# Regrouping the shifted inputs of a state-space stage: a DRAM round trip of five DMAs on GpSimd's queue in place of sixteen identity products per block

## The chip, the cores and the metric

The kernel runs on one core of one Trainium2 chip. The metric is the device time of one launch in microseconds (us). Each version is run several times, and its median is taken. One further execution is recorded by the hardware profiler; the rows below come from it.

## The reference, cut to what matters

Two layers of a decoder trunk on 256 tokens of width 2048, all in float32: layer 0 mixes tokens by stick-breaking attention, layer 1 by a state-space layer (S5), and each is followed by a squared-ReLU MLP. The change lies in the S5 layer alone:

```python
u = h @ w_in                                  # 256 x 2048
ug = u.reshape(B, S, S5_GROUPS, S5_GROUP)     # 128 groups of 16 channels
bur = einsum('btgc,gpc->btgp', u_chunk, bbr)  # and bui: 64 complex states per group
pr, pi, sr, si = associative_scan(combine, (a_r, a_i, bur, bui), axis=1)
y = einsum('btgp,gcp->btgc', hr, cr) - einsum('btgp,gcp->btgc', hi, ci)
y = y + d_skip * u
z = gelu(y)
a, g = split(z @ w_glu, 2)
return a * sigmoid(g)
```

## The kernel before

Activations lie with channels on the partitions: a block is 128 channels (8 S5 groups) by 256 tokens, and there are 16 blocks. The recurrence is not run token by token but in chunks of 4 tokens: the state is updated once per chunk from the chunk's four inputs, and the outputs inside a chunk are made from that state and from short taps on the inputs. For this the inputs of a block are wanted in another form, the tile `imc`: the partition is 32 j + p (p: one of 32 channels of a quarter q; j: the shift in the chunk), and the free dimensions are q (4) and chunk k (65, with one zero column for the chunk before the first).

The stage is `s5_mixer`. Its outer loop runs 8 times over a pair of blocks (`gi`). An iteration multiplies four weight tiles of w_in (`cols_tile`: 24 matmuls each, every weight split into a high and a low part by ScalarE, L130, and VectorE, L132). After each weight tile comes a `tick`, and at a tick the work planned for it by `at(delay, ...)` is issued in the order in which it was planned. So the S5 work of a block is strung over later ticks, between the weight tiles. For block b of a pair, with t = 4 + 2 b counted from the start of the pair:

- t: `s5_expand` (spreads the coefficients, and loads T on SyncE's queue) and `s5_windows`: VectorE takes the finished product out of PSUM times the RMS row (L974), ScalarE adds the shift (L975), both into the tile `u`.
- t + 1: `s5_operands` (L953, L960 on TensorE) and `s5_shuffle`: 16 matmuls with 32 columns of the identity (each runs as two instructions) read `u` in steps of 4 tokens and put the four shifts onto the four partition groups of a PSUM bank (L983). ScalarE copies the bank to `imc` (L985).
- t + 2: `s5_states`: 8 matmuls on `imc` (L998, 16 instructions), then six elementwise operations and one scan on VectorE (L1000 to L1008), giving the states R.
- t + 4: `s5_taps`.
- t + 6: `s5_outputs`: matmuls on R and on `imc` (L1023), then VectorE adds d times u to the product, in `u` (L1024), and ScalarE applies gelu (L1027) into `z`.

Ticks of even and of odd number therefore alternate: at an even tick stand the outputs of one block, the taps of the next and the states of the one after; at an odd tick the operands and the shuffle. `u` and `imc` have three buffers each, so the `u` of a block is free when the gelu of the block three before, issued at the same tick, has read it.

TensorE and GpSimd keep the order in which the program is written (`manual_schedule`). For ScalarE, VectorE and SyncE a scheduler decides the order when the program is compiled. Beside the stage's own work, VectorE has filler: weighted sums for the adaLN vectors of the next sub-layers (L348, L350), on weights `adaw` that SyncE loads. After the stage the GLU follows, whose last weight tiles need the `z` of all 16 blocks (split at L121 and L122); `flush` then issues what is still planned.

Of the kernel before, what the change touches and what calls it, by code (L numbers as in the profile page):

```python
# [8 lines left out]
F32 = mybir.dt.float32  # L9
# [3 lines left out]
AF = mybir.ActivationFunctionType  # L13
OP = mybir.AluOpType
AX = mybir.AxisListType

P = 128
D = 2048
NB = D // P
S = 256  # L20
# [36 lines left out]
class Trunk:  # L57
# [793 lines left out]
    def s5_open(self, sp):  # L851
        g_ = self.nc.gpsimd
        self.sE = sp.tile([P, 2, 4, 4, 2, 16], F32, name="E")
        self.sCA = [sp.tile([P, 2, 4, 4, 2, 16], F32, name="CA%d" % k) for k in range(3)]
        self.sKL = [sp.tile([P, 3, 4, 2, 16], F32, name="KL%d" % k) for k in range(3)]
        self.simc = [sp.tile([P, 4, 65], F32, name="imc%d" % k) for k in range(3)]
        self.sU = [sp.tile([P, 4 + S + 1], F32, name="u%d" % k) for k in range(3)]
        self.sM = [sp.tile([P, 2, 4, 64], F32, name="M%d" % k) for k in range(2)]
        self.sP = [sp.tile([P, 224], F32, name="taps%d" % k) for k in range(2)]
        for t in [self.sE] + self.sP + self.sM + self.sCA + [u[:, 0:4] for u in self.sU]:  # L860
            g_.memset(t, 0.0)
        self.sS = {}

# [104 lines left out]
            nc.tensor.transpose(pk[:, tau * P - P:tau * P], self.sP[bi % 2][:, o:o + P], self.ident)  # L968
        nc.scalar.activation(self.sKL[bi % 3].rearrange("p t q a e -> p (t q a e)"), pk[:, :3 * P], AF.Copy)

    def s5_windows(self, bi, acc):
        nc = self.nc
        uw = self.sU[bi % 3]
        nc.vector.tensor_tensor(uw[:, 4:], acc[:, :S + 1], self.rms, op=OP.mult)  # L974
        nc.scalar.activation(uw[:, 4:4 + S], uw[:, 4:4 + S], AF.Identity, bias=uw[:, 4 + S:])  # L975

    def s5_shuffle(self, bi):
        nc = self.nc
        uw, imc = self.sU[bi % 3], self.simc[bi % 3]
        pi = self.mp()  # L980
        for q in range(4):
            for j in range(4):
                nc.tensor.matmul(pi[32 * j:32 * j + 32, 65 * q:65 * q + 65], self.ident[:, 32 * q:32 * q + 32],  # L983
                                 uw[:, 4 - j:4 - j + 257:4], start=True, stop=True)
        nc.scalar.activation(imc.rearrange("p q k -> p (q k)"), pi[:, :4 * 65], AF.Copy)  # L985

    def s5_states(self, sp, bi):
        nc, s5 = self.nc, self.s5
# [20 lines left out]

    def s5_outputs(self, sp, bi):  # L1010
        nc = self.nc
        u, St = self.sU[bi % 3][:, 4:4 + S], self.sS.pop((bi, "R")).rearrange("p c (q k) -> p c q k", q=4)
        CA, KL, imc = self.sCA[bi % 3], self.sKL[bi % 3], self.simc[bi % 3]
        py = self.mp()
        for tau in range(4):
            for c in range(2 if tau == 0 else 3):
                for q in range(4):
                    o = py[32 * q:32 * q + 32, 64 * tau:64 * tau + 64]
                    if c < 2:
                        lhs, rhs = CA[:, c, q, tau], St[:, c, q]  # L1020
                    else:
                        lhs, rhs = KL[:, tau - 1, q], imc[:, q, 1:65]
                    nc.tensor.matmul(o, lhs.rearrange("p a e -> p (a e)"), rhs, start=(c == 0), stop=(c == (2 if tau else 1)))  # L1023
        nc.vector.scalar_tensor_tensor(u.rearrange("p (k i) -> p i k", i=4), u.rearrange("p (k i) -> p i k", i=4),  # L1024
                                       self.dcol[:, bi:bi + 1], py[:, 0:S].rearrange("p (i k) -> p i k", i=4),
                                       op0=OP.mult, op1=OP.add)
        nc.scalar.activation(self.z[:, bi], u, AF.Gelu_apprx_tanh)  # L1027
        if not self.split_z:
            self.sdone.add(bi)
        else:  # L1030
            self.split(self.hH[:, bi, :S], self.hL[:, bi, :S], self.z[:, bi])

    def s5_mixer(self, mid):
        nc, tc = self.nc, self.tc
        w_in, w_glu = self.i["s5_w_in"][0], self.i["s5_w_glu"][0]
        st = ExitStack()
        sp = st.enter_context(tc.tile_pool(name="s5", bufs=1, reuse_waits="tile"))
        self.z = sp.tile([P, NB, S], F32, name="z")
        self.split_z, self.sdone = False, set()
        hH, hL = self.h()  # L1040
        self.at(1, self.rms_stat, self.sq)
        self.at(3, self.rms_rows)
        self.s5_open(sp)
        self.s5_load(sp, 0)
        for gi in range(8):
            acc = self.accs()
            if gi < 7:
                self.at(2, self.s5_load, sp, gi + 1)
            for b in range(2):
                bi = 2 * gi + b  # L1050
                t = 4 + 2 * b
                self.at(t + 6, self.s5_outputs, sp, bi)
                self.at(t - 0, self.s5_expand, sp, bi)
                self.at(t, self.s5_windows, bi, acc[:, b])
                self.at(t + 1, self.s5_operands, sp, bi)
                self.at(t + 1, self.s5_shuffle, bi)
                self.at(t + 2, self.s5_states, sp, bi)
                self.at(t + 4, self.s5_taps, bi)
            for t in range(4):
                self.cols_tile(acc, w_in, gi * 256, t, hH, hL)  # L1060
        self.open_h(self.pers)
        z = self.h(S)
        for bi in range(16):
            if bi in self.sdone:
                self.split(self.hH[:, bi, :S], self.hL[:, bi, :S], self.z[:, bi])
        self.split_z = True
        self.pace(44, mid[-1])
        sq = self.new_sq()

        def before():  # L1070
            self.flush()
            st.close()
            self.open_h(self.ctx.enter_context(tc.tile_pool(name="h1", bufs=1, reuse_waits="tile")))

        for _ in range(1):
            self.tick()
        a, b = self.gemm_two(w_glu, D, 0, *z, before)
        with tc.tile_pool(name="glu", bufs=2, reuse_waits="tile") as gp:
            for g in range(8):
                if g:  # L1080
                    a = self.gemm_cols(w_glu, D + g * 256, *z)
                sg = gp.tile([P, 2, S], F32, name="sg")
                nc.scalar.activation(sg, a[:, :, :S], AF.Sigmoid)
                if g:
                    b = self.gemm_cols(w_glu, g * 256, *z)
                nc.vector.tensor_tensor(sg, b[:, :, :S], sg, op=OP.mult)
                if g == 5:
                    self.drain(*mid)
                    self.shifts(0, 16, 1, 1)
                    for kb in range(10):  # L1090
                        self.fold(kb, 1, 1)
                for j in range(2):
                    self.residual(sg[:, j], 2 * g + j, 1, 2, sq)
                    if g > 4:
                        self.fold(2 * g + j, 1, 1)
        self.sq = sq
# [128 lines left out]
```

## Time and profile before

| what | us |
|---|---|
| median of 3 runs | 2493.76 (2490.83 to 2493.91) |
| profiled execution, time | 2488.38 |
| profiled execution, span of the trace | 2486.6 |
| TensorE busy | 2374.3 |
| VectorE busy | 1830.0 |
| ScalarE busy | 1207.1 |
| GpSimd busy | 255.6 |

The span is what the trace covers; 1.8 us of the profiled time lie around it. Busy time of an engine is the time in which at least one of its instructions ran; a TensorE that is busy throughout can still be working at less than its fastest, as its matmuls overlap. In the rows, PE is TensorE, PEld its weight loads, DVE is VectorE, ACT ScalarE, POOL GpSimd and SP SyncE; a "q" after the name means the engine's sequencer.

### The profile page before, as it was taken

The numbers are of one execution on the slowest core, as the hardware profiler recorded it, in microseconds if no ns is written. First come the engines' busy times: TensorE is split into PE (matmuls) and PEld (weight loads), VectorE is DVE, ScalarE is ACT, GpSimd is POOL, SyncE is SP. The second block draws the span as 40 slices with busy tenths as digits, with TensorE's granted clock in tenths as the row PEclk, the third lists the DMA queues.
The fourth block names the chain that finished last, engine by engine and source line by source line (L and its number), as shares of the span: only waits on it lengthen the run. The fifth ranks groups of instructions, "written<-read, shape, count | busy, mean of one in ns | idle before, by whom it ended". The sixth has DMA issues, their size and how long they took to land.

```text
span 2486.6 us, 48432 instructions
## 1 busy us (share of the span) xinstructions
PE 2374.3 (95%) x19843; PEld 2234.8 (90%) x19843; DVE 1830.0 (74%) x2479; ACT 1207.1 (49%) x1806; POOL 255.6 (10%) x292
## 2 busy tenths in 40 slices
PE   7999999999999888988999999999999999999998
PEld 4776789899999778888999998999999999999998
DVE  5699999999888878787797699658555555555543
ACT  4534875355444234433546676444543543543543
POOL 0000100000003444454400000000000000000000
PEclk9999999999999989999999999999999999999999
DMA  9898899999998888888898577768555655655654
GB/s 337 301 309 301 289 315 320 334 309 317 320 306 286 274 269 276 262 287 282 279 312 304 179 240 228 230 186 280 177 181 186 184 183 185 185 184 184 185 184 140
DMA packets 503058, 627.28 MB, mean 252 GB/s; under 512 B 44434, under 2 KB 374580, under 8 KB 500532
## 3 DMA queue, kind: packets, MB, share of 16 engines
q1 hardware_dynamic: 499776, 609.31, 75.1%
q0 software_dynamic: 2432, 14.68, 1.5%
q8 instruction: 155, 2.54, 0.4%
q14 instruction: 67, 0.55, 0.1%
q10 hardware_dynamic: 628, 0.21, 0.0%
HBM read 607.34 MB, written 16.78 MB: 251 GB/s over the span
## 4 chain that ended last, share of the span: by engine, by line
PE 58%; DVE 13%; issue 10%; DMA 9%; POOL 7%; ACT 2%; SPq 0%; ACTq 0%; DVEq 0%; POOLq 0%
PE acc L159 14%; PE acc L161 14%; PE acc L160 14%; DMA adaw<-in_ada_w 5%; DVE wl L132 4%; PE acc L145 3%; PE acc L146 3%; PE acc L147 3%; DVE adacc L350 3%; DMA rot<-turns 2%; DVE adsums L350 2%; DMA w<-in_mlp_w 2%; PE mp L291 1%; PE mp L322 1%; ACT wh L130 1%
## 5 line engine op out<-in xcount | busy, mean ns | idle before, releaser
L130 ACT ACTIVATE wh<-w 128x1024 fp32r<-128x1024 f32 x736 | 777.5, 1058 | 1052.9 <-PE acc L161 544.6
L132 DVE TENSOR_TENSOR wl<-w,wh 128x1024 fp32r<-128x1024 f32 x736 | 914.9, 1245 | 409.3 <-ACT wh L130 408.3
L159 PE MATMUL acc<-hH,wl 128*128 128x258 f32 (+1 forms) x2816 | 808.1, 287 | 33.7 <-DVE wl L132 32.2
L161 PE MATMUL acc<-hH,wh 128*128 128x258 f32 (+1 forms) x2816 | 799.5, 284 | 0.0
L160 PE MATMUL acc<-hL,wh 128*128 128x258 f32 (+1 forms) x2816 | 798.0, 283 | 0.5 <-DVE hL L122 0.5
L159 PE MATMUL acc<-aH,wl 128*128 128x256 f32 x2048 | 587.4, 287 | 39.1 <-DVE wl L132 38.4
L160 PE MATMUL acc<-aL,wh 128*128 128x256 f32 x2048 | 581.6, 284 | 0.0
L161 PE MATMUL acc<-aH,wh 128*128 128x256 f32 x2048 | 581.6, 284 | 0.0
L159 PEld LDWEIGHTS acc<-hH,wl 128*128 128x128 f32 x2816 | 535.9, 190 | 48.7 <-DVE wl L132 38.3
L160 PEld LDWEIGHTS acc<-hL,wh 128*128 128x128 f32 x2816 | 536.6, 191 | 0.7 <-DVE hL L122 0.7
L161 PEld LDWEIGHTS acc<-hH,wh 128*128 128x128 f32 x2816 | 535.1, 190 | 0.0
L159 PEld LDWEIGHTS acc<-aH,wl 128*128 128x128 f32 x2048 | 391.0, 191 | 48.5 <-DVE wl L132 47.1
L160 PEld LDWEIGHTS acc<-aL,wh 128*128 128x128 f32 x2048 | 391.1, 191 | 0.0
L161 PEld LDWEIGHTS acc<-aH,wh 128*128 128x128 f32 x2048 | 391.0, 191 | 0.0
L350 DVE SCALAR_TENSOR_TENSOR adacc<-adaw,cond,adacc 128x512 f32<-128x512 f32 x390 | 296.9, 763 | 22.5 <-DMA adaw<-in_ada_w 19.2
L350 DVE SCALAR_TENSOR_TENSOR adsums<-adaw,cond,adsums 128x512 f32<-128x512 f32 x270 | 216.1, 802 | 30.5 <-DMA adaw<-in_ada_w 26.5
L145 PE MATMUL acc<-wh,hL 128*128 128x512 f32 x384 | 156.8, 408 | 5.8 <-ACT wh L130 3.1
L146 PE MATMUL acc<-wl,hH 128*128 128x512 f32 x384 | 153.6, 400 | 3.4 <-DVE wl L132 3.3
L147 PE MATMUL acc<-wh,hH 128*128 128x512 f32 x384 | 152.6, 398 | 0.0
L145 PEld LDWEIGHTS acc<-wh,hL 128*128 128x128 f32 x384 | 73.3, 191 | 32.3 <-issue 13.7
L146 PEld LDWEIGHTS acc<-wl,hH 128*128 128x128 f32 x384 | 72.9, 190 | 21.2 <-DVE wl L132 6.3
L147 PEld LDWEIGHTS acc<-wh,hH 128*128 128x128 f32 x384 | 73.0, 190 | 17.0
(288 smaller groups left out, 2068.9 us busy)
## 6 DMA issues: line engine op xcount, KB each, us to landing
w<-in_mlp_w SPq DMA_DIRECT2D x512, 512.0 KB, 3.9
adaw<-in_ada_w SPq DMA_DIRECT2D x384, 512.0 KB, 5.8
w<-in_sb_w_in SPq DMA_DIRECT2D x96, 512.0 KB, 5.5
w<-in_s_w_glu SPq DMA_DIRECT2D x64, 512.0 KB, 3.9
w<-in_sb_w_out SPq DMA_DIRECT2D x32, 512.0 KB, 5.6
w<-in_s_w_in SPq DMA_DIRECT2D x32, 512.0 KB, 4.6
pw<-W POOLq DMA_DIRECT2D x8, 1024.0 KB, 4.2
W<-pw SPq DMA_DIRECT2D x8, 1024.0 KB, 6.7
```

The source lines that it names most:

```text
L130: nc.scalar.activation(h, w, AF.Copy)
L132: nc.vector.tensor_tensor(l, w, h.bitcast(F32), op=OP.subtract)
L145: nc.tensor.matmul(o, aL(kb)[:, s], H[:, kk], start=(kb == k0), stop=False)
L146: nc.tensor.matmul(o, aH(kb)[:, s], L[:, kk], start=False, stop=False)
L147: nc.tensor.matmul(o, aH(kb)[:, s], H[:, kk], start=False, stop=(kb == k1 - 1))
L159: nc.tensor.matmul(o, L[:, kk, s], aH(kb), start=(kb == k0), stop=False)
L160: nc.tensor.matmul(o, H[:, kk, s], aL(kb), start=False, stop=False)
L161: nc.tensor.matmul(o, H[:, kk, s], aH(kb), start=False, stop=(kb == k1 - 1))
L291: nc.tensor.matmul(st["bank"][32 * kk:32 * kk + 32], self.cond32[:, 4 * t + kk], pair[kk // 2][:, kk % 2], start=(t == 0), stop=(t == 3))
L322: nc.tensor.matmul(st["bank"][32 * i:32 * i + 32], self.ones[:, 0:32], acc, start=True, stop=True)
L350: nc.vector.scalar_tensor_tensor(acc, wt[:, kk], c, acc, op0=OP.mult, op1=OP.add)
```

## The change

The 16 identity products and the copy out of PSUM go. `s5_inputs` takes the place of `s5_windows` and `s5_shuffle`: VectorE writes the scaled product into a tile `uw` of its own; ScalarE, while adding the shift, writes it into `u` with the four tokens of a chunk apart (position first, chunk second). GpSimd's queue stores `u` to a DRAM tile `um` (16 of them, one per block), and four reads on the same queue bring back position (4 - j) mod 4 into the 32 partitions of shift j of `imc`, the shifted ones one column later. The zero columns of `imc` are now set once, by a memset of the three buffers. Since `u` now lies position first, L1024 works on contiguous data, and the gelu writes its result in steps of four tokens. `s5_states` moves from t + 2 to t + 3.

```diff
@@ s5_open
-        self.sU = [sp.tile([P, 4 + S + 1], F32, name="u%d" % k) for k in range(3)]
+        self.sU = [sp.tile([P, S], F32, name="u%d" % k) for k in range(3)]
+        self.um = [self.dram.tile([P, S], F32, name="um%d" % bi) for bi in range(16)]
...
-        for t in [self.sE] + self.sP + self.sM + self.sCA + [u[:, 0:4] for u in self.sU]:
+        for t in [self.sE] + self.sP + self.sM + self.sCA + self.simc:
             g_.memset(t, 0.0)
@@
-    def s5_windows(self, bi, acc):
-        nc = self.nc
-        uw = self.sU[bi % 3]
-        nc.vector.tensor_tensor(uw[:, 4:], acc[:, :S + 1], self.rms, op=OP.mult)
-        nc.scalar.activation(uw[:, 4:4 + S], uw[:, 4:4 + S], AF.Identity, bias=uw[:, 4 + S:])
-
-    def s5_shuffle(self, bi):
-        nc = self.nc
-        uw, imc = self.sU[bi % 3], self.simc[bi % 3]
-        pi = self.mp()
-        for q in range(4):
-            for j in range(4):
-                nc.tensor.matmul(pi[32 * j:32 * j + 32, 65 * q:65 * q + 65], self.ident[:, 32 * q:32 * q + 32],
-                                 uw[:, 4 - j:4 - j + 257:4], start=True, stop=True)
-        nc.scalar.activation(imc.rearrange("p q k -> p (q k)"), pi[:, :4 * 65], AF.Copy)
+    def s5_inputs(self, sp, bi, acc):
+        nc = self.nc
+        uw, u, imc = sp.tile([P, S + 1], F32, name="uw", bufs=1), self.sU[bi % 3], self.simc[bi % 3]
+        nc.vector.tensor_tensor(uw, acc[:, :S + 1], self.rms, op=OP.mult)
+        nc.scalar.activation(u.rearrange("p (i k) -> p i k", i=4), uw[:, :S].rearrange("p (k i) -> p i k", i=4), AF.Identity, bias=uw[:, S:])
+        nc.gpsimd.dma_start(self.um[bi], u)
+        src = self.um[bi].rearrange("(q p) (i k) -> i p q k", q=4, i=4)
+        for j in range(4):
+            o = 1 if j else 0
+            nc.gpsimd.dma_start(imc[32 * j:32 * j + 32, :, o:o + 64], src[(4 - j) % 4])
@@ s5_outputs
-        u, St = self.sU[bi % 3][:, 4:4 + S], self.sS.pop((bi, "R")).rearrange("p c (q k) -> p c q k", q=4)
+        u, St = self.sU[bi % 3], self.sS.pop((bi, "R")).rearrange("p c (q k) -> p c q k", q=4)
...
-        nc.vector.scalar_tensor_tensor(u.rearrange("p (k i) -> p i k", i=4), u.rearrange("p (k i) -> p i k", i=4),
-                                       self.dcol[:, bi:bi + 1], py[:, 0:S].rearrange("p (i k) -> p i k", i=4),
-                                       op0=OP.mult, op1=OP.add)
-        nc.scalar.activation(self.z[:, bi], u, AF.Gelu_apprx_tanh)
+        nc.vector.scalar_tensor_tensor(u, u, self.dcol[:, bi:bi + 1], py[:, 0:S], op0=OP.mult, op1=OP.add)
+        nc.scalar.activation(self.z[:, bi].rearrange("p (k i) -> p i k", i=4), u.rearrange("p (i k) -> p i k", i=4), AF.Gelu_apprx_tanh)
@@ s5_mixer
-                self.at(t, self.s5_windows, bi, acc[:, b])
+                self.at(t, self.s5_inputs, sp, bi, acc[:, b])
                 self.at(t + 1, self.s5_operands, sp, bi)
-                self.at(t + 1, self.s5_shuffle, bi)
-                self.at(t + 2, self.s5_states, sp, bi)
+                self.at(t + 3, self.s5_states, sp, bi)
                 self.at(t + 4, self.s5_taps, bi)
```

## Rows read from the trace of the kernel before

**Rows 1.** Stretches: from:to, us, busy us (instructions) per engine, granted clock, DMA share, GB/s
```profile
1357.00:1446.00 89.00, 89.00 (x1375) 81.73 (x1378) 59.94 (x78) 64.41 (x128) 0.00 (x0) 1.00 0.56 180
1446.00:1545.00 99.00, 97.55 (x1708) 89.46 (x1697) 96.33 (x152) 72.52 (x159) 0.00 (x0) 1.00 0.76 247
1545.00:1572.00 27.00, 25.36 (x425) 24.27 (x424) 25.33 (x37) 10.57 (x15) 0.00 (x0) 0.94 0.84 255
```
**Rows 2.** Timeline of TensorE over one block: start us, us, line, out<-in, count
```profile
1431.04 0.65 PE L953 MATMUL mp<-E,CA 128*32 128x128 f32 x16
1432.64 1.13 PE L983 MATMUL mp<-u,ident 128*32 128x65 f32 x32
1433.69 0.39 PE L159 MATMUL acc<-hH,wl 128*128 128x258 f32 x1
...
1436.77 0.65 PE L1023 MATMUL mp<-R,CA 128*32 128x64 f32 x32
1438.52 1.90 PE L998 MATMUL mp<-imc,VL 128*128 128x64 f32 x16
1440.23 0.37 PE L159 MATMUL acc<-hH,wl 128*128 128x258 f32 x1
...
1443.27 0.62 PE L322 MATMUL mp<-adsums,ones 128*32 128x512 f32 x2
```
**Rows 3.** Source line L983: ns min/median/max, first and last start
```profile
L983 PEldq EVENT_SEMAPHORE  x15: 51/51/51, 1371.4 to 1541.4; - x15
```
**Rows 4.** Timeline of ScalarE and VectorE around the same even tick [idle before <-releaser]
```profile
1439.11 0.68 DVE L1024 SCALAR_TENSOR_TENSOR u<-u,colv,mp 128x256 f32<-128x256 f32 x1
1439.83 0.42 ACT L1027 ACTIVATE z<-u 128x256 f32<-128x256 f32 x1
1442.11 0.51 ACT L975 ACTIVATE u<-u 128x256 f32<-128x256 f32 x1 [1.42 <-DVE u L974]
```
**Rows 5.** Timeline of TensorE and ScalarE at an even tick of the later blocks
```profile
1487.10 0.65 PE L1023 MATMUL mp<-R,CA 128*32 128x64 f32 x32
1491.05 0.42 ACT L1027 ACTIVATE z<-u 128x256 f32<-128x256 f32 x1 [0.59 <-DVE u L1024]
```
**Rows 6.** Timeline of GpSimd in the MLP before: a store, and the instruction that waits for it
```profile
806.33 0.62 POOL L849 DMA_DIRECT2D rot<-turns  x1 [0.31 <-POOL turns L848]
813.47 1.05 POOL L745 TENSOR_TENSOR turns<-s5lo,s5hi 128x256 f32<-128x256 f32 x1 [5.85 <-DMA rot<-turns]
```
**Rows 7.** DMA issues of the whole span: count, KB each, median us to landing
```profile
rot<-turns POOLq DMA_DIRECT2D x16, 384.0 KB, 5.3
T<-rot SPq DMA_DIRECT2D x16, 384.0 KB, 3.8
out<-ot SPq DMA_DIRECT2D x8, 256.0 KB, 2.5
```
**Rows 8.** Tile C (loads of 256-byte runs, 64 KB each, on SyncE's queue): time to landing
```profile
DMA to landing us min/median/max: 2.6/4.0/5.2
```
**Rows 9.** Source lines L418, L1024 and L849: ns min/median/max, first and last start
```profile
L418 DVE SCALAR_TENSOR_TENSOR xT<-acc,mod,xT x112: 469/476/486, 407.7 to 2481.9; 128x256 f32<-128x256 f32 x112
L1024 DVE SCALAR_TENSOR_TENSOR u<-u,colv,mp x16: 667/683/699, 1390.1 to 1564.3; 128x256 f32<-128x256 f32 x16
L849 POOL DMA_DIRECT2D rot<-turns x16: 606/615/623, 806.3 to 1234.1; - x16
```
**Rows 10.** Timeline of SyncE's queue and of VectorE: what the load of T waits for
```profile
1432.32 0.68 DVE L1007 TENSOR_TENSOR w<-R,T 128x512 f32<-128x512 f32 x1
1433.04 0.34 SPq L945 DMA_DIRECT2D T<-rot  x1
```
**Rows 11.** Timeline at the end of the stage: TensorE and VectorE
```profile
1558.75 0.68 DVE L1008 TENSOR_TENSOR R<-w,w 128x512 f32<-128x512 f32 x1
1561.04 0.65 PE L1023 MATMUL mp<-R,CA 128*32 128x64 f32 x32
1565.94 0.38 PE L159 MATMUL acc<-hH,wl 128*128 128x256 f32 x1 [1.14 <-ACT hH L121]
```

## The prediction

> **What bounds the kernel now.** I read the page's busy times first, then the stretches of the S5 stage, then TensorE's timeline inside one block, and last the chain that leads into the work that is moved.
>
> In the stretch of the first seven blocks TensorE is busy for 89.00 of 89.00 us, at the full granted clock, and VectorE for 59.94 [rows 1]. In the stretch of the nine later ones TensorE is busy for 97.55 of 99.00 and VectorE for 96.33: the adaLN filler runs there [rows 1]. So the first part is bound by TensorE alone; in the second VectorE stands close behind. GpSimd does nothing in either.
>
> The reader should see in [rows 2] that a block costs TensorE a fixed sequence with no waits. Even tick: outputs and taps, 1436.77 to 1438.52 (1.75 us), states to 1440.23 (1.71), a weight tile to 1443.27 (3.04). Odd tick: operands 1431.04 to 1432.64 (1.60), the shuffle to 1433.69 (1.05), a weight tile to 1436.77 (3.08). The sum is 12.23 us a block.
>
> **The change, part by part.** The identity products: 16 blocks x 1.05 us of start to start = 16.8 us of TensorE, all on the path. This is the whole of the possible gain that TensorE's rows show.
>
> ScalarE and VectorE: the copy out of PSUM goes (ScalarE, off the path: 64.41 of 89.00 us busy [rows 1]). The gelu and the shift become strided on one side. No row shows a ScalarE operation with steps of four elements; L1024 is one on VectorE, 0.683 us against 0.476 for the same operation on contiguous data [rows 9]. If ScalarE paid the same 0.21 twice it would give back about what the copy cost; at best nothing. I take nothing, under the cover of its idle 28%. L1024 becomes contiguous: about 0.21 less on VectorE per block, 1.9 us in the nine later blocks, where that can count. The memset of `imc` falls on GpSimd while it is idle; were it exposed it would cost about a microsecond once. TensorE's PSUM ring loses one of seven uses per block, which only loosens it.
>
> The new waits: the first state matmul must now wait for four DMAs instead of one ScalarE instruction. A wait that stands as an instruction of its own on TensorE's sequencer took 51 ns [rows 3]. Between none exposed and four per block: 0 to 16 x 4 x 0.051 = 3.3 us; I take 1, as the weight loads run ahead of the matmuls. Behind that wait stands everything on TensorE: the operands of the next block, the next weight tile, and behind these ScalarE's and VectorE's splits.
>
> The DRAM round trip, step by step. ScalarE ends the shift, GpSimd wakes (0.31 [rows 6]), issues the store, waits until it has landed, wakes, issues four reads about 0.65 apart (0.62 each [rows 6]), and the last must land.
> - Store. The nearest row is the other store from GpSimd's queue, three times as large: a median of 5.3 us to landing [rows 7], and 813.47 - 806.33 = 7.1 from the start of the issue to the instruction that waited [rows 6]. A store of twice the bytes from SyncE landed in 2.5 [rows 7]. Bounds 2.5 to 7.1; I take 4.5, nearer to GpSimd's, less something for the bytes.
> - Reads. The nearest row is the loads of 256-byte runs, the same runs as here: 2.6, 4.0 and 5.2 us [rows 8]. I take 4.0.
> - Sum: 0.3 + 4.5 + 0.3 + 3 x 0.65 + 4.0 = 11.05 us; bounds 0.3 + 2.5 + 0.3 + 1.95 + 2.6 = 7.65 and 0.3 + 7.1 + 0.3 + 1.95 + 5.2 = 14.85.
>
> What hides it: the distance from the end of the shift (even tick t) to the states (odd tick t + 3). On TensorE without the shuffle, from the start of the even tick: 1.75 + 3.04, then the odd tick of the block before, 1.71 + 1.60 + 3.08, then 1.75 + 3.04: 15.97 us. The shift can't start before the gelu of three blocks earlier has freed `u`. In the first part that gelu ends at 1440.25, 3.48 after the start of the even tick at 1436.77 [rows 2, 4]; with 0.51 for the shift itself the round trip starts at about 4.2, and 11.8 us are left. In the later blocks the gelu ends 4.37 after it [rows 5], the round trip starts at about 5.1, and 10.9 are left. A shortfall x is not paid in full at each block: the round trip of a block contains the stall of the block before and its own, so each stalls by x / 2. At 11.05 that is 0 in the first seven, and (11.05 - 10.9) / 2 = 0.08 in nine: 0.7 us. At the upper bound it is 7 x 1.5 + 9 x 2.0 = 28.5 us; at the lower bound 0.
>
> Is GpSimd held up when it issues? In the trace an issue there took 0.606 to 0.623 us in all 16 cases [rows 9], in stretches with VectorE at work, so nothing there looks like an issue that was held up. The Trainium skill, "SBUF — State Buffer", section "SBUF: two separate sides", says that DMAs from GpSimd have their descriptors written by that engine, and that certain VectorE operations shut it out meanwhile, so that the DMA seems to hang. By that rule the sum would hold a wait of up to one VectorE operation at each issue; it stands below as a rival.
>
> SyncE: the load of T waits for the last reader of T two blocks before; it went out at 1433.04, as that reader, L1007, ended (1432.32 + 0.68) [rows 10]. With the states one tick later it goes out some 5 us later, and the weight loads behind it on SyncE may too. T is not wanted for another block, and the weights are loaded three tiles ahead, some 6 us a tile. Nothing, unless the compiled order puts T ahead of a late weight: then up to those 5 us once or twice, which I keep for the range.
>
> Later blocks on VectorE: if their filler stays as it is, VectorE needs 96.33 / 99.00 x 12.23 = 11.90 us a block, less 0.21 = 11.69, and TensorE 11.18. Then a block gains 0.54 instead of 1.05, and nine give back 4.6 us. The filler is put in where the compiler sees room, so with shorter blocks less of it should stand there. Between 0 and 4.6 I take 2.
>
> The end of the stage: the states of the last block, too, come one tick later, but its outputs don't. L1008 of that block ended at 1559.43 and the outputs ran at 1561.04 [rows 11], 1.6 us of slack. A tick there is 3 us of TensorE, so the outputs wait 1.4 more, up to 3 with filler in between; the GLU's last tiles already waited 1.14 for the split of `z` behind them [rows 11]. I take 1.5.
>
> Sum: -16.8 + 1.0 + 0.7 + 2.0 + 1.5 = -11.6 us. Against the profiled execution: 2488.4 - 11.6 = 2476.8. The median of the runs lies 5.4 above it, so the median forecast is 2493.8 - 11.6 = 2482.2 us, say 2482.
>
> **The rivals.**
> - The round trip is half hidden. For it: five DMAs in two dependent steps, where one such store alone has taken 7.1 us. Against it: that store was three times the size, in a busier stretch. At 13 us the stalls are 7 x 0.6 + 9 x 1.05 = 13.7 in place of 0.7; with the later blocks held by TensorE's stalls the filler costs nothing more (-2): -11.6 + 13.0 - 2 = about -1, 2493.
> - The round trip is not hidden, and the kernel is slower. Place: the first state matmul of each block. It decides from the point where the stalls pass 14.3 us in all (16.8 less the 2.5 of waits and tail), about 0.9 a block: a round trip over 11.3 + 1.8 = 13.1 us on average. At the upper bound of 14.85 the sum is -16.8 + 1.0 + 28.5 + 1.5 = +14, 2508.
> - GpSimd's issues are held up by VectorE, one operation of about 0.7 us [rows 9] at each of the five: 3.5 us more, a round trip of 14.55, stalls of (7 x 2.75 + 9 x 3.65) / 2 = 26 us, +12, 2506. The even issue times speak against it. It is what the rule of the Trainium skill, above, would make of this kernel.
> - VectorE holds the later blocks in full: 4.6 in place of 2, and the tail at 3: -16.8 + 1 + 0.7 + 4.6 + 3 = -7.5, 2486.
>
> **How the numbers follow.** Hidden, as in the sum: 0.45. VectorE holds the later blocks: 0.15. Half hidden: 0.20. Not hidden: 0.15. Held-up issues: 0.05. The forecast is that of the likeliest, 2482. Upwards the range reaches through the half-hidden case to where the last two begin to weigh, 2500; downwards to the case in which nothing is given back (16.8) and VectorE's 1.9 counts, 2475. A difference of 0.2% (5 us) is about what can be told from none here. Faster by more than that: 0.45 + 0.15 less a little for misses of size, 0.57; within it: most of the half-hidden case, 0.20; slower: 0.23.
>
> **What would show it.** If right: TensorE's timeline shows operands followed directly by the weight tile and about 11.2 us a block in the first part; the four reads land before the first state matmul, and no wait of L998 on `imc` stands among the waits. If wrong by the round trip: TensorE idle in front of L998 with a DMA as releaser, of similar size at each block. If wrong by VectorE: L159 waiting for `wl` in the later blocks only. If wrong by held-up issues: DMA issues on GpSimd well over 0.62 us, or long gaps between issue and first byte beside VectorE's operations.

## The result, and the profile after

| kernel | median, us | lowest to highest |
|---|---|---|
| before | 2493.84 | 2490.83 to 2495.97 |
| changed | 2508.36 | 2501.04 to 2510.51 |

The changed kernel takes 1.0052 times as long as the one before (95% interval 1.004 to 1.0064), that is 14.5 us more, where 11.6 less was forecast. Its profiled execution has a span of 2508.2 us against 2486.6. The difference arises in the S5 stage: from the first operand matmul to the last outputs it is 1362.6 to 1586.3, 223.7 us, where the kernel before took 201.2 (1360.9 to 1562.1). So 22.5 us are to be explained there, and they include the gain of the products that went.

In the changed kernel the lines have other numbers: L975 is VectorE's product into `uw`, L976 the shift on ScalarE, L977 the store of `um`, L981 the four reads into `imc`, L954 and L961 the operands, L994 the state matmuls, L996 to L1004 the states on VectorE, L1019 the outputs, L1020 d times u, L1021 the gelu.

The stretches of the stage, with the columns of [rows 1]:

```profile
1357.00:1446.00 89.00, 82.47 (x1095) 78.22 (x1094) 54.87 (x72) 62.57 (x117) 19.14 (x35) 0.92 0.60 187
1446.00:1565.00 119.00, 105.72 (x1493) 98.73 (x1492) 91.18 (x145) 78.34 (x157) 22.44 (x41) 0.87 0.66 210
1565.00:1594.00 29.00, 26.22 (x417) 24.95 (x416) 24.39 (x36) 11.34 (x16) 2.17 (x4) 0.88 0.68 202
```

Two columns have changed. TensorE (the first busy time) was never idle in the first 89 us before, and now is for 6.5 us there and for 13.3 in the next stretch. And the granted clock, 1.00 before, is 0.92, 0.87 and 0.88. As the clock has two levels, 1.00 (2.4 GHz) and 0.50 (1.2 GHz), 0.87 over 119 us means 2 x 0.13 x 119 = 31 us at the lower one.

What TensorE waits for in the stage (us in total, times, longest):

```profile
PE mp L994 <- DMA imc<-um: 20.4, 7, 4.7
```

This is the mark that the prediction named for "wrong by the round trip". One block, on TensorE, to be laid beside [rows 2]:

```profile
1415.26 0.65 PE L1019 MATMUL mp<-R,CA 128*32 128x64 f32 x32
...
1433.33 3.64 PE L994 MATMUL mp<-imc,VL 128*128 128x64 f32 x16 [2.33 <-DMA imc<-um]
1436.91 1.08 PE L954 MATMUL mp<-E,CA 128*32 128x128 f32 x16
1437.92 1.97 PE L961 MATMUL mp<-ident,E 128*128 128x128 f32 x8
1439.54 0.54 PE L159 MATMUL acc<-hH,wl 128*128 128x258 f32 x1
```

The wait of 2.33 us is one thing; what follows is another. The states, 1.71 us from start to start in [rows 2], take 1433.33 to 1436.91 = 3.58, and the operands 2.63 in place of 1.60. The clock over the same moments, in short stretches:

```profile
1431.00:1433.30 2.30, 0.01 (x1) 0.00 (x0) 0.43 (x1) 1.32 (x2) 0.56 (x1) 0.96 0.80 274
1433.30:1437.00 3.70, 3.67 (x20) 3.58 (x24) 0.00 (x0) 0.00 (x0) 1.61 (x3) 0.50 0.08 19
1437.00:1440.00 3.00, 3.00 (x26) 2.58 (x27) 2.98 (x4) 0.95 (x3) 0.57 (x2) 0.51 0.13 33
1440.00:1445.00 5.00, 5.00 (x119) 4.77 (x119) 4.25 (x6) 4.65 (x10) 0.00 (x0) 1.00 0.62 176
```

TensorE does nothing for 2.3 us, and then works for 6.7 us at 1.2 GHz. States and operands together lost (3.58 + 2.63) - (1.71 + 1.60) = 2.9 us on top of the 2.33.

The round trip of that block, and the start of the next one's, on ScalarE, SyncE and GpSimd:

```profile
1418.65 0.66 ACT L1021 ACTIVATE z<-u 128x256 f32<-128x256 f32 x1
1419.35 0.76 ACT L976 ACTIVATE u<-uw 128x256 f32<-128x256 f32 x1
1418.66 0.93 SPq L867 DMA_DIRECT2D W<-pw  x1
1420.39 0.56 POOL L977 DMA_DIRECT2D um<-u  x1 [8.41 <-ACT u L976]
1427.68 2.17 POOL L981 DMA_DIRECT2D imc<-um  x4 [6.73 <-PE mp L1019]
...
1431.67 0.56 POOL L977 DMA_DIRECT2D um<-u  x1 [1.81 <-ACT u L976]
1435.39 2.17 POOL L981 DMA_DIRECT2D imc<-um  x4 [3.16 <-issue]
```

The shift ends at 1420.11; the store is issued 0.28 later; 7.29 us after the start of its issue the reads go out; the state matmuls start 5.65 after that. Together 13.2 us, of which 2.33 are the wait. The next block's store was followed by its reads after 3.72 us, and its states didn't wait. GpSimd's timeline gives this distance from store to reads for all 16 blocks: 2.6, 7.3, 4.9, 4.7, 3.2, 7.3, 3.7, 7.0, 4.9, 6.7, 3.0, 8.1, 5.2, 4.9, 2.5, 3.9 us. Slow are blocks 1, 5, 7, 9 and 11 (counted from 0; the one above is block 5), with 6.7 to 8.1: the odd ones, at which SyncE loads W, the 1 MB of coefficients for a later pair. Its issue stands 1.05 to 1.76 us ahead of the store in blocks 5 to 11, as above at 1418.66, and 0.42 behind it in block 1; where it was 3.0 ahead (block 3), the store took 4.7.

The DMA issues of the stage (count, KB each, median us to landing) and the operations that the change touched (ns min/median/max):

```profile
W<-pw SPq DMA_DIRECT2D x6, 1024.0 KB, 7.9
um<-u POOLq DMA_DIRECT2D x16, 128.0 KB, 4.4
imc<-um POOLq DMA_DIRECT2D x64, 32.0 KB, 3.8
...
L976 ACT ACTIVATE u<-uw x16: 732/754/782, 1361.3 to 1560.1; 128x256 f32<-128x256 f32 x16
L1021 ACT ACTIVATE z<-u x16: 654/666/679, 1395.0 to 1588.3; 128x256 f32<-128x256 f32 x16
L1020 DVE SCALAR_TENSOR_TENSOR u<-u,colv,mp x16: 473/476/481, 1393.2 to 1587.8; 128x256 f32<-128x256 f32 x16
L977 POOL DMA_DIRECT2D um<-u x16: 542/561/563, 1362.4 to 1561.1; - x16
```

### The profile page after: what moved, and what is told of

It reads as the page before. It is cut to its first block, busy times and chain, and to the rows that moved or that the text cites. A ratio compares the mean times of both kernels' runs of the same rounds, so it can differ in the third digit from the quotient of the medians.

```text
span 2508.2 us, 47541 instructions
## 1 busy us (share of the span) xinstructions
PE 2373.8 (95%) x19331; PEld 2237.7 (89%) x19331; DVE 1825.5 (73%) x2479; ACT 1209.9 (48%) x1790; POOL 300.7 (12%) x372
## 4 chain that ended last, share of the span: by engine, by line
PE 58%; DMA 12%; DVE 11%; issue 10%; POOL 7%; ACT 2%; SPq 0%; DVEq 0%; POOLq 0%; ACTq 0%
PE acc L159 14%; PE acc L161 14%; PE acc L160 14%; DMA adaw<-in_ada_w 6%; DVE wl L132 4%; PE acc L146 3%; PE acc L145 3%; PE acc L147 3%; DVE adacc L350 3%; DMA w<-in_mlp_w 2%; DMA rot<-turns 2%; PE mp L994 2%; DMA imc<-um 1%; DVE adsums L350 1%; ACT wh L130 1%
## 5 line engine op out<-in xcount | busy, mean ns | idle before, releaser
L130 ACT ACTIVATE wh<-w 128x1024 fp32r<-128x1024 f32 x736 | 776.8, 1058 | 1036.6 <-PE acc L161 506.8
```

The costliest lines, as they stand in the source:

```text
L130: nc.scalar.activation(h, w, AF.Copy)
```

## The experiments

**Three terms that add up.** For each kernel the table has the length of the stage against the 201.2 us of before (first operands to last outputs), TensorE's idle time in it and the time for which TensorE worked at the lower clock, both counted over the stage in stretches of half a microsecond. The worked-out column is: -20.5 for the products, where they are gone (1.28 a block, see the next section); plus the idle time less the 1.5 of before; plus half of the time at the lower clock, since work takes twice as long there; plus 8 x 2.4 = 19.2 for unread matmuls, where they were put in. This is book-keeping: it says how much of the stage was idle or slow, not why. The last column is the ratio of the medians.

| kernel | stage | idle | at 1.2 GHz, working | worked out | ratio (95%) |
|---|---|---|---|---|---|
| changed | +22.5 | 21.8 | 45.3 | +22.5 | 1.0052 (1.004 to 1.0064) |
| b_states_late | +0.1 | 2.1 | 0 | +0.6 | 0.999 (0.9978 to 1.0003) |
| a_prev_imc | -18.9 | 2.8 | 0 | -19.2 | 0.9924 (0.9903 to 0.9945) |
| a_no_w | +0.5 | 12.5 | 19.1 | 0.0 | 1.0011 (0.9996 to 1.0027) |
| a_store_act | +5.2 | 14.7 | 23.6 | +4.5 | 1.001 (0.9997 to 1.0023) |
| a_fill | +14.9 | 8.7 | 16.9 | +14.4 | 1.0046 (1.0028 to 1.0063) |
| b_fill | +17.5 | 0.0 | 0 | +17.7 | 1.0063 (1.005 to 1.0076) |
| a_t4 | +0.8 | 17.6 | 8.8 | 0.0 | 1.0011 (0.9995 to 1.0026) |
| a_u4 | -11.0 | 6.1 | 8.2 | -11.8 | 0.9951 (0.9929 to 0.9972) |
| a_u4_act | -16.9 | 4.0 | 0 | -18.0 | 0.9946 (0.9929 to 0.9963) |
| a_u4_act2 | -13.1 | 5.5 | 6.1 | -13.5 | 0.9955 (0.994 to 0.997) |

The worked-out column meets the measured stage within 1.1 us in every row. For the changed kernel it reads -20.5 + 20.3 + 22.65: waiting cost about as much as the products had, and the lower clock after the waits as much again. Outside the stage the executions differ without any edit: the stage starts at 1360.9 us in the profile of before and at up to 1376.7 (a_t4) in the others. So a span is not to be set against a span here: the changed kernel's profile is 21.6 us above that of before, its median 14.5.

**b_states_late: the move of the states alone.** The kernel before, with the states one tick later.

```diff
-                self.at(t + 2, self.s5_states, sp, bi)
+                self.at(t + 3, self.s5_states, sp, bi)
```

> The kernel before, with its identity products, and only the states one tick later. Theory (the loss sits in the DRAM round trip): the tick alone costs little, the tail's 1 to 3 us: 2494 to 2497, no wait in front of the state matmuls. Rival (the tick is what costs, by its order of work on VectorE and SyncE): near the changed kernel, 2503 to 2510.

Measured: 2492.16 against 2493.56, 0.999 (0.9978 to 1.0003). The move costs nothing, at the end of the stage either.

**a_prev_imc: the wait alone taken away.** The changed kernel with all its DMAs, but the state matmuls read the `imc` of the block before, which has long been there. What the states compute is changed by that.

```diff
-        VL, imc, T = self.sS.pop((bi, "VL")), self.simc[bi % 3], self.sS.pop((bi, "T"))
+        VL, imc, T = self.sS.pop((bi, "VL")), self.simc[(bi + 2) % 3], self.sS.pop((bi, "T"))
```

> The changed kernel, but the state matmuls read the imc of the block before, which has long landed; this changes what is computed in the states. All DMAs still run. Theory (the wait for the DMAs is the whole loss): TensorE has no wait in front of the states, the clock stays at 1.00 in the stage, and the identity products' 16.8 us come out less the tail: 2478 to 2484. Rival (the DMAs' traffic, the strided ScalarE operations or VectorE cost as such): 2490 or more.

Measured: 2475.97 against 2493.56, 0.9924, two microseconds below the range that was expected, which took 16.8 us for the products. The stretch of the later blocks, columns as above:

```profile
1446.00:1565.00 119.00, 115.37 (x1889) 109.87 (x1889) 116.40 (x184) 87.64 (x170) 24.18 (x44) 1.00 0.83 259
```

The 80 DMAs are there, TensorE has its full clock back, and 17.6 us are gained. So the loss lies in the wait for `imc` and in what follows from it; the traffic itself, GpSimd and ScalarE's steps of four cost nothing that can be seen when nobody waits for them.

**a_no_w: the stores without W beside them.** The coefficients of the pair two before are used again, so the six loads of W are left out.

```diff
+        if gi > 1:
+            self.sS[gi] = self.sS[gi - 2]
+            return
```

> The changed kernel without the loads of W (1 MB) for pairs 2 to 7: these take the coefficients of two pairs before, so the stage computes something else. Theory (the store of an odd block lands late because W is being loaded beside it: 6.9 us from store to reads with a W load, 3.8 without): all stores take 2.5 to 5 us, the stalls of odd blocks fall under 2 us or go: 2482 to 2494. Rival (the store is slow for another reason, the weights or GpSimd's queue): odd blocks keep 6 to 8 us, 2502 to 2508.

Measured: 2492.23 against 2491.52, 1.0011. GpSimd's timeline (here L980 is the store and L984 the reads), over two odd blocks and the even one between them:

```profile
1405.14 0.56 POOL L980 DMA_DIRECT2D um<-u  x1 [6.72 <-ACT u L979]
1407.68 2.17 POOL L984 DMA_DIRECT2D imc<-um  x4 [1.98 <-DMA um<-u]
1414.94 0.56 POOL L980 DMA_DIRECT2D um<-u  x1 [5.08 <-ACT u L979]
1418.34 2.17 POOL L984 DMA_DIRECT2D imc<-um  x4 [2.84 <-PE mp L964]
1425.67 0.56 POOL L980 DMA_DIRECT2D um<-u  x1 [5.16 <-ACT u L979]
1428.20 2.18 POOL L984 DMA_DIRECT2D imc<-um  x4 [1.97 <-PE mp L964]
```

From store to reads it is 2.5, 3.4 and 2.5 us. The mean of the odd blocks from 3 to 11 is 3.7 in place of 6.8. So it is the load of W that held up the stores of these blocks, in the main: blocks 9 and 11 still take 4.8 and 5.1. Block 1 is different: it takes 6.4 without W where it took 7.3, so something else held it up. The Trainium skill, "DMA: Bandwidth & Descriptors", section "Queues, rings and completion order", says that a DMA engine takes turns between the queues that it has work for, a packet at a time; that a small store is slowed by a large load on another queue agrees with it. Without W, waits of 11.1 us for the DMAs are left in front of the states, where they were 20.4, and 3.8 and 4.2 of them stand at blocks 0 and 13, which have no W beside their store in the changed kernel either. So W makes up about half of the waiting, and not all of it.

**a_store_act: the store from another queue.** Only the queue that issues the store is changed.

```diff
-        nc.gpsimd.dma_start(self.um[bi], u)
+        nc.scalar.dma_start(self.um[bi], u)
```

> The changed kernel with the store issued from ScalarE's queue, right behind the shift, and the four reads on GpSimd's as now. Theory (traffic decides how late the store lands): odd blocks keep about 6 us from store to reads, 2500 to 2508. Rival (GpSimd's queue is what makes the store slow): all stores land a microsecond or more sooner, most stalls go, 2485 to 2495.

Measured: 2494.12 against 2491.52, 1.001. ScalarE's queue and GpSimd at an odd block:

```profile
1412.97 0.75 ACT L976 ACTIVATE u<-uw 128x256 f32<-128x256 f32 x1
1413.74 0.33 ACTq L977 DMA_DIRECT2D um<-u  x1
...
1420.41 2.17 POOL L981 DMA_DIRECT2D imc<-um  x4 [11.72 <-DMA um<-u]
```

The issue takes 0.33 us in place of 0.56, and the wake-up of GpSimd (0.28) is gone: half a microsecond. The store to reads is still 6.7 at this odd block, and 6.2 in the mean of the odd blocks from 3 to 11, where it was 6.8. So the time is the one that was expected of the rival, while most of the store's delay stayed, as the theory had it. The stage is 17 us shorter than in the changed kernel: the idle time fell by 7.1, the time at the lower clock by 21.7. An earlier store is worth more than its half microsecond, because the clock comes back with the waits that go; how much of the 7.1 that half microsecond made, and how much the loads beside it, this run does not separate.

**a_fill and b_fill: work put into the gap.** 20 unread matmuls (128 x 128 by 128 x 256) ahead of the states of each odd block, in the changed kernel and, as the control, in the one before.

```diff
+        if bi % 2:
+            pd = self.mp()
+            for _ in range(20):
+                nc.tensor.matmul(pd[:, :S], self.hH[:, 0, :P], self.hH[:, 0, :S], start=True, stop=True)
```

> The changed kernel with 20 extra matmuls of the weight tile's form (0.12 us each, 2.4 us; their result is read by nothing) ahead of the states of each odd block, the blocks that stall. Theory (half of the loss is TensorE at 1.2 GHz after each stall: 8 stretches, 51 us, against 3.4 us before): the stalls shrink to 0 to 2.3 us, most of the low stretches go, and the time falls though TensorE has 19 us more to do: 2490 to 2500. Rival (the idle time alone is the loss): the filler only fills the wait, 2506 to 2514.

> The kernel before, with the same 20 unread matmuls ahead of the states of the eight odd blocks that the changed kernel was given in an earlier run. Here TensorE has no gap at that place. If unread matmuls cost what TensorE's rows show for them, the stage grows by 8 x 2.4 = 19 us: about 2512, a ratio of 1.0077, and TensorE stays without a stall ahead of the states and at the full granted clock. If instead they overlap with what stands around them (so that they are cheap anywhere, and their costing nothing in the changed kernel says nothing of its gaps), the ratio stays under 1.002.

Measured: 1.0046 in the changed kernel (2502.85, between the two cases that were expected, as 8.7 us of idling stayed), no more than the 1.0052 without the matmuls, and 1.0063 in the kernel before (2507.6 against 2492.57, 15.0 us; the expected 19 is the upper end of the interval). TensorE at the same place, first in the control (L998 the unread matmuls, L1002 the states), then in the changed kernel (L994 and L998):

```profile
1436.84 2.64 PE L998 MATMUL mp<-hH 128*128 128x256 f32 x20
1439.32 1.89 PE L1002 MATMUL mp<-imc,VL 128*128 128x64 f32 x16
```

```profile
1434.02 2.56 PE L994 MATMUL mp<-hH 128*128 128x256 f32 x20
1436.41 1.90 PE L998 MATMUL mp<-imc,VL 128*128 128x64 f32 x16
1438.24 0.64 PE L954 MATMUL mp<-E,CA 128*32 128x128 f32 x16
```

Both groups take 2.4 to 2.5 us from start to start. In the control they are pure cost. In the changed kernel 19 us more of TensorE cost nothing: they stand where it would have waited, and behind them the states take 1.90 and not 3.64, as the clock has not fallen. This is the plainest evidence for the second half of the loss. The idle time fell by 13.1 us only, so 6.1 of the 19.2 should still show; that the stage became 7.6 us shorter instead is the clock's doing, with 28.4 us less of work at 1.2 GHz.

**a_t4: one more tick of distance.** The states at t + 4; the storage that this takes comes from R in one buffer, states computed in place, and `uw` kept in an unused part of `z`.

```diff
-                self.at(t + 3, self.s5_states, sp, bi)
+                self.at(t + 4, self.s5_states, sp, bi)
...
-        R = self.sS[bi, "R"] = sp.tile([P, 2, 256], F32, name="R", bufs=2)
+        R = self.sS[bi, "R"] = sp.tile([P, 2, 256], F32, name="R", bufs=1)
```

> The changed kernel with the states at t + 4, one more tick of some 4.8 us for the round trip, with the buffers that this needs (VL 2, KL 2, R 1, VectorE's states in place). Theory: all stalls in front of the states go, apart from the first blocks; the tail costs 2 to 4 us more: 2480 to 2488. Rival (a longer distance only moves the stall, to the outputs that wait for R, or VectorE bounds the later blocks): 2494 or more, with L1018 or L159 as the waiting line.

Measured: 2494.97 against 2493.56, 1.0011. TensorE's waits, and its timeline at one block:

```profile
PE mp L1018 <- DVE R L1003: 17.6, 10, 5.8
...
1502.46 0.65 PE L1018 MATMUL mp<-R,CA 128*32 128x64 f32 x32 [0.97 <-DVE R L1003]
...
1503.82 2.00 PE L993 MATMUL mp<-imc,VL 128*128 128x64 f32 x16
```

The state matmuls no longer wait for the DMAs, but the outputs wait for VectorE's R: with less time between states and outputs the wait has moved. R in one buffer may have its part in that; no run separates the two. The wait is nearly as long, but six of its ten pieces are of 0.8 to 1.0 us; the 8.8 us of work at the lower clock, in place of 45.3, all come behind the last two pieces, of 2.4 and 5.8 us. So the time comes out level with before.

**a_u4: an earlier start.** `u` in four buffers, so that the shift needn't wait for the gelu of three blocks before; `uw` again in `z`.

```diff
-        self.sU = [sp.tile([P, S], F32, name="u%d" % k) for k in range(3)]
+        self.sU = [sp.tile([P, S], F32, name="u%d" % k) for k in range(4)]
...
-        uw, u, imc = sp.tile([P, S + 1], F32, name="uw", bufs=1), self.sU[bi % 3], self.simc[bi % 3]
+        uw, u, imc = self.z[:, bi], self.sU[bi % 4], self.simc[bi % 3]
```

> The changed kernel with u in four buffers (and uw kept in the still unused part of z), so that the shift no longer waits for the gelu of three blocks before. Theory (the round trip is a few us too long): the store goes out 2 to 3 us earlier after the start of the even tick than the 5.1 to 6.6 us now, the stalls of 2 to 4.7 us shrink, and many no longer pull the clock down: 2485 to 2495. Rival (the store's time to land decides, and the compiled order leaves the shift where it is): 2503 to 2510.

Measured: 2482.01 against 2493.56, 0.9951 (0.9929 to 0.9972). The even tick and the states on TensorE, and the shift and the store:

```profile
1415.41 0.65 PE L1019 MATMUL mp<-R,CA 128*32 128x64 f32 x32
1417.08 0.76 ACT L976 ACTIVATE u<-z 128x256 f32<-128x256 f32 x1 [0.15 <-DVE z L975]
1418.14 0.56 POOL L977 DMA_DIRECT2D um<-u  x1 [7.89 <-ACT u L976]
...
1420.05 1.89 PE L994 MATMUL mp<-imc,VL 128*128 128x64 f32 x16
...
1426.37 0.66 PE L1019 MATMUL mp<-R,CA 128*32 128x64 f32 x32
```

The shift ends 1417.84 - 1415.41 = 2.4 us after the start of the tick, where in the changed kernel it ended 1420.11 - 1415.26 = 4.85 after it. With 2.4 us more cover the states don't wait here, and a block takes 1426.37 - 1415.41 = 10.96 us against 12.23 before. Of the waits for the DMAs 5.1 us are left, 4.0 of them at 1384.84, at the first block. The time is 3 us better than the range that was expected.

**a_u4_act, and again as a_u4_act2: both together.** Four buffers of `u` and the store from ScalarE's queue.

> u in four buffers (as before) and the store on ScalarE's queue: GpSimd no longer holds the store of one block behind the wait for the store of the other (with four buffers alone the second store of a pair went out right behind the reads of the first, 5 us late). Theory: the first block's stall of 4.0 us and the 0.8 later go: 2477 to 2481. Rival: ScalarE's issue of the store delays its own work, and nothing is won: 2482 to 2486.

> The changed kernel with four buffers of u and the store on ScalarE's queue once more, in more rounds, beside the control. If the distance alone is what the change lacked, it stays 0.4 to 0.7% faster than before (about 2480), with no stall of over 1 us ahead of the states and no stretch of the stage at the lower clock. If its lead was one of the chip, the ratio comes back within 0.2% of 1.

Measured: 0.9946 (0.9929 to 0.9963), and the second time 2479.81 against 2492.57, 0.9955 (0.994 to 0.997). In the second profile two waits for the DMAs are left, the first of them at the first states (1373.44), the other near the end of the stage (1541.40):

```profile
PE mp L994 <- DMA imc<-um: 2.9, 2, 1.5
```

So this version and a_u4 are faster than both kernels, by half a per cent than the one before; that no wait above 1 us and no work at the lower clock would be left was too much (6.1 us of it in the second profile).

## Why the prediction was wrong

**The products: right, and under-rated.** 16 x 1.05 = 16.8 us were taken from the shuffle's own rows. Without it a block takes 10.96 us (a_u4) against the 12.23 of [rows 2]; over eleven blocks (from the states of block 1 to those of block 12) it is 11.09 in a_prev_imc against 12.37 before, 1.28 less, which makes 20.5 in all. Most of the difference to 1.05 lies at a seam: after L961 the next weight tile starts 0.85 us after L961's start in a_u4 (1411.51 to 1412.36), where after the same group the shuffle started 1.02 later (1407.14 to 1408.16 before).

**The step that failed first: the landing of the store.** 4.5 us were taken for "store", from rows of stores in other stages, with 7.1 as the upper bound. Even blocks took 2.5 to 5.2 from store to reads; five of the six odd ones beside a load of W took 6.7 to 8.1, at that bound and past it. With reads issued and landed as worked out (four issues in 2.17 us, a median landing of 3.8), the round trip came to 13.2 in place of 11.05. The working took the store from its row and its size, in a stage that it held to be less busy, and did not ask which load would be in flight when it went out; the load of W stands on SyncE's queue in the trace of before too (at 1416.24, for one).

**The distance.** "11.8 us are left" was 10.9 at the block shown (1420.11 to the 1431.00 at which the states could have begun). ScalarE's steps of four were costed at nothing "under the cover of its idle 28%". They cost 0.25 us at the gelu (0.666 against 0.42, [rows 4]) and 0.25 at the shift (0.754 against 0.51), and both stand on the path from the even tick to the store. An engine's idle share covers nothing when the operation is on the chain that is waited for. As to the rest, the gelu began 0.33 later after the tick than in [rows 2, 4] (3.39 against 3.06), though its input was ready at 1418.07: ScalarE was still at work on coefficients. And from the even tick to the states it was 15.74 in place of 15.97. The "about 4.2" had 0.2 to spare. VectorE's L1020 gave 0.21 back as worked out (476 ns against 683, [rows 9]).

**The stall rule.** A shortfall x was priced at x / 2 per block, on equal blocks. The blocks are not equal. TensorE idled ahead of the states of blocks 0, 3, 5, 7, 9, 11, 13 and 15, for 2.8, 1.4, 2.3, 1.9, 2.1, 4.6, 4.7 and 2.0 us (the profile puts the 1.4 down to ScalarE's L130, the others to the DMAs). The odd blocks from 3 to 11 have W beside their store: there the odd block pays in full (13.2 - 10.9 = 2.3 us at the block shown), and this lets the even one through without a wait. But 9.5 us were idled away at blocks 0, 13 and 15, which have no W beside them. At block 13 it is the distance that is short:

```profile
1531.84 0.77 ACT L976 ACTIVATE u<-uw 128x256 f32<-128x256 f32 x1
...
1539.89 0.55 PE L969 MATMUL mp<-ident,taps 128*128 128x128 f32 x3
1545.12 3.65 PE L994 MATMUL mp<-imc,VL 128*128 128x64 f32 x16 [4.69 <-DMA imc<-um]
```

The shift ends at 1532.61 and the states could have begun at 1540.43, 7.8 us later and not 10.9: this tick stands behind the last weight tile of w_in, and no weight tile lies between its taps and the states. The round trip was 12.5 us, shorter than at the block shown above. The total of 20.4 us is inside the range that the upper bound gave (28.5).

**The term that was missing: the clock.** No step priced what TensorE does after a wait. In the changed kernel idle times of 1.4 to 4.7 us, eight of them, were each followed by work at 1.2 GHz, 45.3 us in all, which cost 22.6 us: more than the waits, and more than the products gave. It was put at nothing without a reason, and it decided: without it the terms come to -20.5 + 20.3 = -0.2 us, which is the half-hidden rival. With it, the case "not hidden" decides far earlier than at the 13.1 us of its working, as a microsecond of waiting cost about two on the whole. [Rows 11] had a hint: the stretch at the end of the stage, with a wait of 1.14, is the only one of [rows 1] whose clock is under 1.00.

**The rival that came closest.** "The round trip is not hidden" gave 2508 for the upper bound of the sum, and 2508.36 was measured. Its place was right, the first state matmul, and its cause as well, DMAs as releaser. That its price met the median is luck. In the profiled stage waits and slow work took 20.3 + 22.65 us where it had 28.5, the products gave 20.5 where it had 16.8, and its 2.5 for waits and tail weren't found: +22.5 against its +14. The medians differ by only 14.5, as the profiled execution lies 5.5 us under its median before and 1.7 above it after the change.

**Right, or of no weight.** The move of the states and the tail: 1.5 us were taken for it, and b_states_late shows none; the wait for the split of `z` is 0.56 where it was 1.14 [rows 11].

```profile
1589.47 0.38 PE L159 MATMUL acc<-hH,wl 128*128 128x256 f32 x1 [0.56 <-ACT hH L121]
```

VectorE, taken at 2 us, doesn't hold the later blocks: in a_prev_imc it is busy for 116.40 of 119 us and the stage is still 18.9 shorter. Held-up issues had a chance of 0.05 and don't occur: the store's issue took 0.542 to 0.563 us in all 16 cases. The rule of the Trainium skill ("SBUF — State Buffer", section "SBUF: two separate sides") that GpSimd's DMAs are shut out by certain VectorE operations is not borne out by any row of this stage, though no row tells whether VectorE ran the operations that it means.

**What stays open.** Why some even blocks took 4.9 and 5.2 us from store to reads, without W beside them, and block 1 as long as 6.4 in a_no_w; adaLN weights and w_in are loaded there too, and no run took those away. And whether an order of SyncE's loads with W later would do as much as a_no_w: that wasn't tried.

## What to carry to other kernels

When a step leaves the engine that bounds the stage for a chain of DMAs, work out the chain from what is in flight at that moment, not from medians, count each operation on the chain at its full price, however idle its engine is, and look at the first and last blocks by themselves. Where waits of TensorE like these (1.4 to 4.7 us) are to be feared, price them at about twice their length, as they came to here (20.3 us of waits and 22.6 of slower work); so a margin of two microseconds, here one more buffer, turned a loss of 0.5% into a gain of 0.5%. And a removed step is worth the difference of the period, not its own rows: seams come with it.

## What the runs showed of the hardware

- Short waits cost the clock: after a single idle time of TensorE of 2.33 us, 6.7 us ran at 1.2 GHz; over the stage 21.8 us of idling were followed by 45.3 us of such work. The cost is not in proportion to the idling: in a_t4 17.6 us of it, mostly in smaller pieces, were followed by 8.8 us of such work, and in a_u4_act 4.0 us by none. Idle times of 1.4 and 1.9 us in the changed kernel were each followed by 3.4 us of slow work, but one of 1.8 in a_store_act and two of 1.8 and 2.0 in a_t4 by none.
- A store of 128 KB from GpSimd's queue landed in a median of 4.4 us; from store to reads it was 3.7 us in the mean of the odd blocks from 3 to 11 without the 1 MB load beside it, and 6.8 with it.
- Steps of four elements on one side cost ScalarE 0.25 us on 128 x 256 float32 (0.666 against 0.42, 0.754 against 0.51), about what they cost VectorE (0.683 against 0.476).
- An issue on ScalarE's queue took 0.33 us, on GpSimd's 0.56.
